# An output projection by block products: seven per pair of token tiles instead of eight

## The chip, the cores and the metric

The kernel runs on one core of a Trainium2 chip. A core has five engines that run side by side, each with its own queue in order: TensorE (PE, matmuls, with a queue of weight loads PEld), VectorE (DVE), ScalarE (ACT), GpSimd (POOL) and SyncE (SP, which here issues all the DMAs). The metric is the device time of one launch in microseconds (us), here the median of three runs.

## The reference

The reference is one layer of a streaming encoder: a modulated RMS norm, one input projection, a state-space branch and an attention branch, and then the output projection, which is what the change touches:

```
mixed = jnp.concatenate([y_ssm, y_att], axis=-1)
y = x + gate[:, None, :] * (mixed @ w_out)
```

`mixed` has 1024 channels (512 of the state-space branch, 512 of attention), for 2048 prompt tokens and 64 decode tokens. `w_out` is 1024 x 1024. All data are float32.

## The kernel before

The program goes through the input projection with the state-space steps between (class `InProj`, `S5`), a gated projection (`Glu`), attention (`Attn`, lines 995 to 1387) and the output projection (`Out`, from line 1480). Both branches leave their outputs, transposed, in DRAM: `ms_d` and `ma_d`, each 512 channels by 2112 tokens.

A float32 product is formed from halves: `split` (line 277) rounds a tile to a high part (float32r) and subtracts it from the tile to get a low part. `mm3` (line 308) then issues three matmuls, high by high, high by low and low by high. A stationary operand is 128 x 128, a moving one 128 x 512.

`Out.weights` (line 1489) is a generator that attention steps through near its end: each step loads a 128 x 512 block of `w_out` into one of three `ost` buffers, rounds it on DVE (`oh`) and subtracts on POOL (`ol`). It takes memory that attention no longer needs. `Out.run` (line 1503) then goes over 17 token tiles, tile 16 (decode) first and then 15 down to 0. For each it loads 128 tokens of `ms_d` and of `ma_d`, splits them on DVE, and for each half of the 1024 output columns runs 8 x 3 matmuls into one accumulator, multiplies by the gate on DVE (line 1531), adds the residual on POOL (`padd`, line 174) and stores.

Attention goes over 20 query tiles, five for each of four pairs of heads. A tile's keys come in blocks, two blocks a group: scores on PE into a `twin`, `p` = exp on ACT (line 304), the sums `acc` over the blocks (line 1297) alternately on DVE and POOL, and one group later the product of `p` with the values (`mix`, into `bank`). At the end of a tile the two `acc` are joined on POOL (line 1379), a matmul against ones sums over the keys (`sums`), and the result `w` is stored to `ma_d` (line 1324). For the very last tile only (`end`), the last six blocks and the join are on DVE (line 1284).

PE's order in attention is the order written (`Chain`, `strict`). Everything else, and the whole output projection, is ordered on each engine by a planner at build time, from estimated costs and dependencies, with the written order as priority. So instructions of the output projection stand among those of attention, as in the first `ost` loads, which go out more than 100 us before attention ends.

## Time and profile before

| | us |
|---|---|
| median of 3 runs | 1456.5 (1455.73 to 1466.12) |
| the profiled execution, whole | 1460.03 |
| its span, first to last instruction | 1458.3 |
| mean granted clock of TensorE | 0.979 |
| first matmul of the output projection | at 1264.94 |
| its last matmul | at 1452.80 |

The profile is of one execution. Times in it count from the first instruction. A group line reads: line, engine, operation, output from inputs, shape, count, then busy time and mean ns of one, then the engine's idle time just before and what ended it. A timeline line reads: start, duration, engine, line, operation, and in brackets the idle time before it and what it waited for. A line of stages gives the stage, then for PE, PEld, DVE, ACT and POOL the busy time and (count), then the granted clock, the DMA share and GB/s. L124 is the helper that all matmuls pass through, so matmuls are told apart by their tiles.

### The profile page before, as it was taken

What the parts mean: (1) busy time and instruction counts of PE and PEld (TensorE: products, weight loads), DVE (VectorE), ACT (ScalarE), POOL (GpSimd) and SP (SyncE); (2) the same over time, 40 slices, a digit from 0 to 9 for tenths busy, and PEclk for the clock granted to TensorE, in tenths of its full rate; (3) what the DMA queues carried; (4) which work ended last, traced back from release to release, by engine and by line L of the source; (5) the groups of instructions that cost most, each with busy time, mean ns of one, the idle gap of its engine ahead of it and who ended that gap; (6) DMA issues with size and microseconds to landing.
All of it is one profiled execution on the core that took longest, in us unless ns stands there. A gap on an engine that the chain in (4) does not pass through costs nothing. (4 is left out here: it accounts for less than half of the span.)

```text
span 1458.3 us, 26193 instructions
## 1 busy us (share of the span) xinstructions
PE 1374.8 (94%) x9730; PEld 1082.7 (74%) x9730; DVE 909.4 (62%) x2406; ACT 541.5 (37%) x1156; POOL 480.5 (33%) x452
## 2 busy tenths in 40 slices
PE   5899989999999999999999999999999897999998
PEld 2798889889888889998878855555555454478887
DVE  2646898678767795564214777886886877342331
ACT  3755215343433444333324435445445344300000
POOL 1101356235322362231125413423324527322222
PEclk9999999999999999999999989999999999999999
DMA  9875423323335725235458623133121222054452
GB/s 336 297 274 150 120 65 85 103 81 89 114 88 165 259 77 139 67 98 148 132 169 252 183 93 107 45 98 93 55 74 38 87 63 91 23 159 147 136 150 94
DMA packets 209383, 184.01 MB, mean 126 GB/s; under 512 B 66823, under 2 KB 169955, under 8 KB 208232
## 3 DMA queue, kind: packets, MB, share of 16 engines
q1 hardware_dynamic: 209256, 182.35, 40.8%
q8 instruction: 76, 1.25, 0.4%
q14 instruction: 51, 0.42, 0.1%
HBM read 125.16 MB, written 57.15 MB: 125 GB/s over the span
## 5 line engine op out<-in xcount | busy, mean ns | idle before, releaser
L124 PE MATMUL low<-whi,h 128*128 128x256 f32 (+1 forms) x2112 | 406.9, 289 | 12.7 <-DVE ev L534 7.3
L124 PEld LDWEIGHTS low<-whi,h 128*128 128x128 f32 x2112 | 337.4, 193 | 23.2 <-issue 11.9
L124 PE MATMUL low<-wlo,h 128*128 128x256 f32 (+1 forms) x1088 | 307.9, 286 | 0.6 <-DVE wlo L284 0.6
L1220 DVE CUSTOM_DVE_ANT_0 pb<-twin,cb 128x512 bf16<-128x512 f32 (+3 forms) x328 | 199.7, 609 | 62.8 <-PE twin L124 51.4
L124 PEld LDWEIGHTS low<-wlo,h 128*128 128x128 f32 x1088 | 209.2, 192 | 2.2 <-issue 1.2
L304 ACT ACTIVATE p<-twin 128x1024 f32<-128x1024 f32 (+3 forms) x180 | 150.0, 839 | 146.1 <-PE twin L124 137.4
L124 PE MATMUL low<-h,whi 128*128 128x512 f32 (+1 forms) x640 | 176.7, 362 | 0.0
L124 PE MATMUL bank<-p,vt 128*64 128x512 f32 (+3 forms) x704 | 143.6, 530 | 0.0
L124 PE MATMUL twin<-qs,ks 64*128 64x512 f32 (+3 forms) x1056 | 134.2, 359 | 0.0
L124 PEld LDWEIGHTS low<-h,whi 128*128 128x128 f32 x640 | 115.0, 192 | 17.7 <-issue 1.7
L290 POOL TENSOR_TENSOR qss<-qss,mhalf 128x4 f32<-128x4 f32 (+1 forms) x68 | 77.2, 1137 | 143.0 <-DVE qss L289 118.9
L124 PE MATMUL low<-h,wlo 128*128 128x512 f32 (+1 forms) x320 | 115.4, 361 | 0.0
L284 DVE TENSOR_TENSOR wlo<-wst,whi 128x512 fp32r<-128x512 f32 (+1 forms) x96 | 67.8, 718 | 76.2 <-ACT whi L282 73.5
L1297 DVE TENSOR_TENSOR acc<-acc,p 128x1024 f32<-128x1024 f32 (+4 forms) x89 | 87.5, 983 | 28.7 <-ACT p L304 27.1
L124 PEld LDWEIGHTS twin<-qs,ks 64*128 64x128 f32 x1056 | 95.2, 191 | 10.9
L124 PE MATMUL twin<-sm,kb 64*128 64x512 f32 (+3 forms) x360 | 78.0, 428 | 17.5 <-DVE pm L1220 17.0
L124 PEld LDWEIGHTS bank<-p,vt 128*64 128x64 f32 x704 | 45.4, 141 | 65.6 <-issue 56.2
L175 POOL TENSOR_TENSOR yo<-yo,x 128x512 f32<-128x512 f32 (+1 forms) x34 | 49.0, 1441 | 133.6 <-DVE yo L1531 133.6
L124 PE MATMUL last<-oh,mh 128*128 128x512 f32 (+1 forms) x208 | 81.4, 391 | 0.0
L124 PE MATMUL last<-ol,mh 128*128 128x512 f32 (+1 forms) x208 | 81.1, 390 | 0.0
L124 PE MATMUL last<-oh,ml 128*128 128x512 f32 (+1 forms) x208 | 81.1, 391 | 0.0
L124 PEld LDWEIGHTS twin<-sm,kb 64*128 64x128 f32 x360 | 34.6, 188 | 60.4 <-DVE pm L1220 40.0
(365 smaller groups left out, 2503.8 us busy)
## 6 DMA issues: line engine op xcount, KB each, us to landing
wst<-in_w_in_dram SPq DMA_DIRECT2D x48, 512.0 KB
h<-h SPq DMA_DIRECT2D x16, 1024.0 KB
wada<-in_w_ada_dram SPq DMA_DIRECT2D x12, 1024.0 KB
cb<-cb_d SPq DMA_DIRECT2D x20, 512.0 KB
x<-in_x_prompt_dram SPq DMA_DIRECT2D x16, 512.0 KB
out_dram<-ev SPq DMA_DIRECT2D x64, 128.0 KB
x<-in_x_prompt_dram SPq DMA_DIRECT2D x32, 256.0 KB
out_dram<-yo SPq DMA_DIRECT2D x32, 256.0 KB
```

What stands on the lines that cost most here:

```text
L124: return self.keep(self.pe.matmul(*a, **kw))
L175: PL.tensor_tensor(out, x, y, op=op)
L284: V.tensor_tensor(lo, x, hi, op=ALU.subtract)
L290: PL.tensor_tensor(out, out, bc(mhalf[:out.shape[0]], list(out.shape)), op=ALU.pow)
L304: i = S.activation(out, x, func, **kw)
L1220: V.tensor_tensor_reduce(b[:, :n], ps[:, h, :n], cb[:, h, :n], 1.0, NEG, ALU.add, ALU.max, accum_out=self.pm[:, t, h, pi:pi + 1])
L1297: (PL if j else V).tensor_tensor(y[:rows, :, c0:nq], x[:rows, :, c0:nq], p[:rows, :, :n], op=ALU.add)
```

## The change

`w_out` is seen as 2 x 2 blocks b11, b12, b21, b22 (512 channels by 512 columns each), and a pair of token tiles with its two branches as 2 x 2 blocks too: a11, a21 (state-space channels of the first and the second tile), a12, a22 (attention channels). Eight block products give the four results. For pairs 1 to 7 the kernel now forms seven, of sums and differences: s1 = a21 + a22, s2 = s1 - a11, s3 = a11 - a21, s4 = a12 - s2 on one side; t1 = b12 - b11, t2 = b22 - b12 + b11, t3 = b22 - b12, t4 = b21 - t2 on the other (`PRODUCTS`). Three accumulators x, y, z are held for a pair, some products add onto what another left, and DVE combines them. Pair 0 is done with four plain products of blocks (`plain`), and the 64 decode tokens with high and low parts side by side in one stationary operand (`decode`).

`w_out` is loaded once as before, rounded now on ACT, and a second time for the sums and differences (`sums`), which `part` splits later; t3 and t4 take the place of b12's halves. Residuals come as whole rows of 1024. A pair's `ms_d` and `ma_d` come in two loads of 256 tokens, issued ahead of the last two stores of the pair before; their buffers are single. High parts of the pairs are rounded on ACT, low parts are on DVE, s1 and s3 on POOL. The pairs run upward, 0 to 7. The last result of the last pair has its residual and an earlier sum added ahead and its last add on DVE.

Inside the output projection the order on each engine is now the written one (`ordered`). In attention, the last two tiles, not only the last, have their last six sums and the join on DVE; the steps of `weights` begin once the last maxima are placed too; and the memory that is free after attention is found by what is in use (`fill`). The core of the diff:

```diff
+    def ordered():
+        start = len(nc.cur_bb.bb.instructions)
+        yield
+        last = {}
+        for i in nc.cur_bb.bb.instructions[start:]:
+            if i.engine in last:
+                tc.add_manual_dep(i, last[i.engine], nosync)
+            last[i.engine] = i.name
...
-                                   given=[False, False], n=0, nb=len(blocks), po=None, end=i == len(self.order) - 1)
+                                   given=[False, False], n=0, nb=len(blocks), po=None, end=i >= len(self.order) - 2)
...
-                if not self.todo and not self.loaded and not self.mx:
+                if not (self.todo or self.loaded or self.mx or self.smq):
...
-        out.mem.add(self.spare("cb", "ks", "qs", "sm", "vt") + self.ring("p", "acc", "z", "w"))
+        out.mem.fill(0, R_AUP[1])
...
+    PRODUCTS = {1: ("x", "a11", "b11"), 2: ("x", "a12", "b21"), 3: ("z", "s4", "b22"), 4: ("y", "a22", "t4"),
+                5: ("z", "s1", "t1"), 6: ("y", "s2", "t2"), 7: ("y", "s3", "t3")}
...
+                st = mem.tile([P, 512], F32, name="ost")
+                e.nc.sync.dma_start(st, self.block(i, j, k))
+                h, l = (mem.tile([P, 512], F32R, name="o%s%d%d%d" % (x, i, j, k)) for x in "hl")
+                e.split(st, h, l)
...
+        self.load(0)
+        for name in ("a11", "a12", "a21", "a22"):
+            self.split(0, name)
+            yield
...
+        for k in range(4):
+            yield from wait(4)
+            for i, j in blocks[1:]:
+                x = self.raw[i, j, k] = mem.tile([P, 512], F32, name="r%d%d%d" % (i, j, k))
+                e.nc.sync.dma_start(x, self.block(i, j, k))
+            b11 = self.raw[0, 0, k] = mem.tile([P, 512], F32, name="ost")
+            e.nc.sync.dma_start(b11, self.block(0, 0, k))
+            self.raw["t", k] = mem.tile([P, 512], F32, name="rt%d" % k)
+            self.sums(k)
+            yield
...
+    def sums(self, k):
...
+        e.V.tensor_tensor(b22, b22, b12, op=ALU.subtract)
+        e.V.tensor_tensor(t2, b22, b11, op=ALU.add)
+        e.padd(b12, b12, b11, ALU.subtract)
+        e.padd(b21, b21, t2, ALU.subtract)
...
+    def part(self, t):
+        for k in range(4):
+            x, lo = self.raw[t, k]
+            if t in ("t3", "t4"):
+                hi = self.b["b12", k][t == "t4"]
+            else:
+                hi = self.mem.tile([P, 512], F32R, name="h%s%d" % (t, k))
+            self.e.split(x, hi, lo, el=None if t == "t3" else self.e.V)
+            self.b[t, k] = hi, lo
...
+    def finish(self, i, n, v, src=None, last=False):
...
+        e.V.tensor_tensor(v[:r], (v if src is None else src)[:r], self.gate[s, n][:r], op=ALU.mult)
+        if last:
+            e.V.tensor_tensor(x, x, v[:r], op=ALU.add)
+        else:
+            e.padd(x, x, v[:r])
+        e.nc.sync.dma_start(e.y_p[t0:t0 + r, ns] if s == 0 else e.y_s[:, ns], x)
...
+        self.multiply(acc, self.a[p, a], b, first)
+        if n == 1:
+            t[p, 1] = self.temp()
+            S.copy(t[p, 1], acc)
+        if n in (1, 6) and (p, 1) in t and (p, "y") in self.acc:
+            t[p, 2] = self.temp()
+            V.tensor_tensor(t[p, 2], self.acc[p, "y"], t[p, 1], op=ALU.add)
+        if n == 7:
+            t[p, 3] = self.temp()
+            V.tensor_tensor(t[p, 3], acc, t[p, 1], op=ALU.add)
+            V.tensor_tensor(t[p, 3], t[p, 3], self.acc[p, "z"], op=ALU.add)
+            self.finish(2 * p + 1, 1, t[p, 3])
...
+        self.residual(16)
+        self.load(1)
+        for i in range(2):
+            self.residual(i)
+        self.decode(1)
+        self.decode(0)
+        self.part("t1")
+        self.differ(1, 1)
+        self.differ(1, 3)
+        self.differ(1, 2)
+        self.differ(1, 4)
+        self.plain(0, 1)
+        self.part("t2")
+        self.plain(0, 0)
+        self.split(1, "s2", "a11", "s1", "a12")
+        self.plain(1, 1)
+        self.part("t3")
+        self.part("t4")
+        self.split(1, "s3", "a22")
+        self.load(2)
+        for i in range(2, 4):
+            self.residual(i)
+        self.plain(1, 0)
+        for p in range(1, 8):
+            q = p + 1 if p < 7 else 0
+            self.split(p, "s4")
+            if q:
+                self.differ(q, 1)
+                self.differ(q, 3)
+            self.product(p, 6)
+            self.product(p, 1)
+            if q:
+                for i in (2 * q, 2 * q + 1):
+                    self.residual(i)
+            self.product(p, 5)
+            if q:
+                self.differ(q, 2)
+                self.differ(q, 4)
+                self.split(q, "s2", "a11")
+            self.product(p, 7)
+            if q:
+                self.split(q, "s1", "a22")
+            self.product(p, 2)
+            if q:
+                self.split(q, "s3", "a12")
+                if q < 7:
+                    self.load(q + 1)
...
+            self.product(p, 3)
+            self.product(p, 4)
```

More of the change, by code (lines that the diff above doesn't have):

```diff
@@ L1485, in __init__ @@
         self.mem = Region(e.nc)
[L1486 to L1487 removed]
+        self.b, self.a, self.x, self.acc, self.tmp, self.raw = {}, {}, {}, {}, {}, {}
+        self.d = []
     def weights(self):
         e = self.e
[L1492 to L1501 removed]
@@ new lines, in split, with multiply @@
+    def split(self, p, *names):
+        for name in names:
+            hi, lo = (self.mem.tile([P, 4, P], F32R, tag="m" + x + name, name="m" + x) for x in "hl")
+            self.e.split(self.a[p, name], hi, lo, el=self.e.V)
+            self.a[p, name] = hi, lo
+    def multiply(self, acc, a, b, first=True):
+        ah, al = a
+        for k in range(4):
+            bh, bl = self.b[b, k]
+            for q, (lhs, rhs) in enumerate(((ah, bh), (ah, bl), (al, bh))):
+                self.e.PE.matmul(acc, lhs[:, k], rhs, start=first and k == q == 0, stop=k == 3 and q == 2,
+                                 skip_group_check=True)
@@ L1615, in body @@
         out.ps = Banks(e.banks(top, "last", 6) + e.psum, *range(8))
-        out.run([16] + list(range(15, -1, -1)))
+        with e.ordered():
+            out.run()
 _INS = ["x_prompt", "x_sample", "cache_k", "cache_v", "cache_logf", "state_ssm_re", "state_ssm_im", "c_prompt",
```

184 lines of the change are left out of this document (142 added, 42 removed).

## The prediction

> **What bounds the kernel now.** I read the page's head first, then the busy time by stages, the chain of waits for the last 300 us, the groups of instructions of the output stage, and the timeline of each engine around the end of attention.
>
> ```profile
> span 1458.3 us, 26193 instructions
> PE 1374.8 (94%) x9730; PEld 1082.7 (74%) x9730; DVE 909.4 (62%) x2406; ACT 541.5 (37%) x1156; POOL 480.5 (33%) x452
> GB/s 336 297 274 150 120 65 85 103 81 89 114 88 165 259 77 139 67 98 148 132 169 252 183 93 107 45 98 93 55 74 38 87 63 91 23 159 147 136 150 94
> 1300.00:1400.00 100.00, 100.00 (x441) 82.50 (x440) 32.50 (x57) 0.00 (x0) 27.05 (x19) 1.00 0.48 145
> 1311.23 32.76 PE last L124 x144
> L124 PE MATMUL last<-oh,mh 128*128 128x512 f32 x192 | 75.0, 391 | 0.0
> L124 PE MATMUL bank<-oh,mh 128*128 128x512 f32 x64 | 25.0, 390 | 0.0
> L124 PE MATMUL last<-oh,mh 128*64 128x512 f32 x16 | 6.4, 398 | 0.0
> ```
>
> The fourth line is a stretch of the output projection: PE is busy for all 100 us at full clock (1.00), DVE for 32.5, POOL for 27, ACT for none, and the DMA engines for 48% at 145 GB/s. So this stage is bound by TensorE, and a matmul left out is time saved. The fifth line, from the chain of waits, prices one: 32.76 / 144 = 0.2275 us (the 391 ns of the groups overlap the next matmul). The last three lines are one operand form each; the forms with ol and with ml have the same counts, so the stage has 3 x (192 + 64 + 16) = 816 matmuls, 185.6 us.
>
> The second place is in attention, ahead of that stage.
>
> ```profile
> 1231.96 0.43 DVE L280 CAST oh<-ost 128x512 fp32r<-128x512 f32 x1 [2.07 <-DMA ost<-in_w_out_dram]
> 1232.30 2.08 DVE L1297 TENSOR_TENSOR acc<-acc,p 128x512 f32<-128x512 f32 x2
> 1232.46 1.64 POOL L175 TENSOR_TENSOR ol<-ost,oh 128x512 fp32r<-128x512 f32 x1 [3.39 <-DVE oh L280]
> 1234.53 2.34 POOL L1379 TENSOR_TENSOR acc<-acc,acc 128x1024 f32<-128x1024 f32 x1 [0.43 <-DVE acc L1297]
> 1236.92 1.98 PE L124 MATMUL bank<-acc,ones 128*64 128x512 f32 x4 [6.39 <-POOL acc L1379]
> 1238.68 3.63 PE L124 MATMUL bank<-p,vt 128*64 128x512 f32 x8
> 1244.30 1.94 PE L124 MATMUL bank<-p,vt 128*64 128x512 f32 x8
> 1268.98 1.03 PE L124 MATMUL bank<-acc,ones 128*64 128x512 f32 x4
> 1237.00:1243.00 6.00, 6.00 (x18) 1.82 (x20) 2.63 (x3) 1.23 (x2) 5.72 (x3) 0.56 0.18 52
> ```
>
> PE stands idle for 6.39 us. Followed back: DVE waits for a block of w_out, rounds it, only then adds the softmax sums of the last but one query tile, POOL splits that block and then joins the two sums, and the matmul against ones waits for it. Afterwards the granted clock is 0.56: the same two groups take 1.98 and 3.63 us instead of 1.03 and 1.94. The place costs 6.4 + 0.95 + 1.69 = 9.0 us. [...]
>
> **The matmuls.** For tokens 256 to 2047 a pair of token tiles takes 7 block products of 12 matmuls instead of 2 x 48: 84 for 96. Tokens 0 to 255 keep four plain blocks of 24. The 64 decode tokens put high and low halves side by side into one stationary operand: 2 x 16 instead of 48. Together 7 x 84 + 96 + 32 = 716 for 816: 100 x 0.2275 = 22.75 us less. All of this counts as long as the operands are ready in time; that is the turnover below.
>
> **The last but one tile.** Its last six blocks and the join go to DVE, and rounding w_out goes from DVE to ACT. POOL's join (2.34 us) and the DVE rounding that held the sums are both off this path. I take the whole 9.0 us, less what ACT brings in:
>
> ```profile
> 1251.32 1.94 ACT L304 ACTIVATE p<-twin 128x1024 f32<-128x1024 f32 x2 [1.91 <-PE twin L124]
> 1239.57 0.63 ACT L304 ACTIVATE w<-w 128x512 f32<-128x512 f32 x1
> PE twin L124 <- DVE pm L1220: 7.6, 9, 2.5
> 1225.35 1.45 DVE L280 CAST oh<-ost 128x512 fp32r<-128x512 f32 x1 [2.29 <-DMA ost<-in_w_out_dram]
> 1240.00:1260.00 20.00, 20.00 (x126) 9.51 (x122) 7.17 (x6) 8.83 (x10) 10.34 (x5) 0.94 0.04 14
> ```
>
> In each group of two key blocks ACT works 1.94 us and idles 1.91 (first line). A copy from SBUF of the same size takes 0.63 (second), so two per group fit: no cost. But ACT runs in order: a copy that waits for its DMA as DVE did (2.29 us, fourth line) holds the exponentials behind it, and PE's next mix waits for those. Ends: 0, and the eight copies of the last eight groups by (2.29 + 0.63 - 1.91) = 8 us. Since a mix runs only after the next group's scores, most of that is covered; I take 1 us. The gain side has an end too: between 1140 and 1270 PE waited 7.6 us, in nine places, for DVE's maxima (third line), and DVE's rounding of w_out stands in that queue; with it gone up to 7.6 us could fall away. I take none, since POOL's halves of the same blocks stay and the order around them is free to change.
>
> **The tail.**
>
> ```profile
> 1452.80 0.39 PE L124 MATMUL last<-oh,ml 128*128 128x512 f32 x1
> 1453.29 0.69 DVE L1531 TENSOR_TENSOR yo<-last,gate 128x512 f32<-128x512 f32 x1 [4.75 <-PE last L124]
> 1454.06 1.26 POOL L175 TENSOR_TENSOR yo<-yo,x 128x512 f32<-128x512 f32 x1 [4.16 <-DVE yo L1531]
> 1455.34 0.34 SPq L1533 DMA_DIRECT2D out_dram<-yo  x1
> ```
>
> Behind the last matmul stand DVE 0.69, POOL 1.26, the store. Now the sum of the last two old terms is done ahead, and the last add is on DVE at 0.69 or less: -0.65 us. The store before it now comes 2.7 us earlier instead of 5.5 us, still ahead of the last one.
>
> **One pair in the steady state.** PE needs 84 x 0.2275 = 19.1 us. What the other engines do beside it:
>
> ```profile
> L284 DVE TENSOR_TENSOR ml<-m,mh 128x512 fp32r<-128x512 f32 x31 | 21.3, 687 | 1.6
> 1289.55 0.68 DVE L1531 TENSOR_TENSOR yo<-last,gate 128x512 f32<-128x512 f32 x1
> 1290.14 0.68 DVE L284 TENSOR_TENSOR ml<-m,mh 128x512 fp32r<-128x512 f32 x1
> 1290.31 1.67 POOL L175 TENSOR_TENSOR yo<-yo,x 128x512 f32<-128x512 f32 x1 [3.08 <-DVE yo L1531]
> 1295.74 1.28 POOL L175 TENSOR_TENSOR yo<-yo,x 128x512 f32<-128x512 f32 x1 [3.76 <-DVE yo L1531]
> 1211.83 2.06 DVE L1297 TENSOR_TENSOR acc<-acc,p 128x1024 f32<-128x1024 f32 x1
> 1244.54 1.23 DVE L1297 TENSOR_TENSOR acc<-acc,p 128x1024 f32<-128x1024 f32 x1 [4.92 <-ACT p L304]
> 1212.76 2.27 POOL L175 TENSOR_TENSOR w<-w,z 128x512 f32<-128x512 f32 x1
> ```
>
> DVE: 7 low halves, 2 differences, 9 combining and gate instructions: 18 x 0.687 = 12.4 us. POOL: 2 differences and 4 residual adds: 6 x 1.28 = 7.7. ACT: 7 high halves and a copy: 8 x 0.63 = 5.0. All are under 19.1. But DVE and POOL delay each other when both read SBUF: an add that POOL does alone in 1.28 took 1.67 beside a DVE subtraction, a DVE add of 1.23 took 2.06 beside POOL. [...] Wholly one after the other they need 20.1 us a pair, 1.0 more than PE; six of DVE's 18 read a PSUM operand, though, so 16.0 is nearer. The first operand that the next pair needs shows the room: product 1 ends 5.5 us into a pair, then come ACT's copy (0.63), DVE's sum, two differences and s2's low half (4 x 0.69), so s2 is ready at about 9 and used at 19.1. So I take 0; ends 0 and 7 x 1.0 = 7.
>
> Accumulators are reused inside a pair: product 7 adds onto a bank that DVE must have read, and products 2, 3 and 4 likewise. Between write and reuse lies at least one product (2.73 us) and the reading needs 0.6 + 0.7: covered. On SP the loads of the next pair stand ahead of the last two stores and behind residual loads that wait for earlier stores; none is needed sooner than about 6 us later.
>
> **The turnover.** Here the change adds most: w_out is read a second time (16 blocks, 4.2 MB), its sums and differences are formed, and four sums are split. PE has cover: 32 decode and 96 plain matmuls, 29.1 us, then three products, 8.2, before the first product 7. DVE and POOL must by then have done, counted from the code: DVE 35 instructions with SBUF operands (4 low halves of pair 0, 8 sums, 4 + 4 + 4 low halves of t1, t2, t4, 2 differences and 7 low halves of pair 1, 2 gate products) and POOL 20 (8 sums, 2 differences, 6 residual adds, 4 low halves of t3).
>
> ```profile
> 1272.71 0.32 SPq L1324 DMA_DIRECT2D ma_d<-w  x1
> 1274.77 0.37 SPq L1513 DMA_DIRECT2D m<-ma_d  x1
> 1277.58 0.49 DVE L280 CAST mh<-m 128x512 fp32r<-128x512 f32 x1 [1.16 <-DMA m<-ma_d]
> ```
>
> 35 x 0.687 + 20 x 1.28 = 49.6 us one after the other against 37.3 of cover. Little of it can be done earlier: in 1240 to 1260 DVE and POOL together were busy 17.5 of 20 us. The second reading can't start in full before attention's buffers are free; at the page's first rate (336 GB/s) its 4.2 MB take 12.5 us, at the output stage's (145) 29. One of the gate loads goes into a buffer that the last attention store must have left (2.1 us from store to next load, first two lines), and pair 1 is queued behind it on SP; a load then takes 2.8 us to its first use. Ends: 0, if work before the turnover and overlap cover the 12.3 us excess, and 15, if nothing does and PE then restarts at 0.56 clock. DVE instructions issued in a row start every 0.59 us (1289.55 and 1290.14 above) rather than 0.69, which takes 3 off the excess; a part of the sums can run in attention's last 15 us. I take 4.
>
> **Sum.** Against the profiled execution (1458.3 span + 1.7 around it = 1460.0): -22.75 - 9.0 - 0.65 + 1 + 4 = -27.4, 1432.6. The median of the runs, 1456.5, is 3.5 below that execution; from it: 1429.
>
> **Rivals.**
> 1. The wait at 1236 only moves: a copy on ACT behind a late w_out block takes 8 to 9 us. For it: the 2.29 us DMA wait that DVE had. Against: the 1.91 us idle in each group. 1429 + 8.5 = 1437.5.
> 2. The turnover starves PE: the whole 15 instead of 4, 1440; with half of ACT's 8 on top, 1444. For it: 49.6 against 37.3. Against: the overlap.
> 3. Attention gives more: with rounding off DVE the earlier waits for maxima go as well. 1429 - 7.6 = 1421.4. For it: one queue. Against: most of those waits stand behind DVE's own maxima, which stay.
> 4. Slower: pair loads have one buffer, so the load of pair q+2 waits for the last low half of pair q+1, and the differences wait for the load. If load (6 us for 1 MB) and 20.1 us of DVE and POOL run strictly in turn, a pair takes 26.1, 7.0 more than PE's: 1429 + 49 = 1478. It decides from 23.0 us a pair, where 7 x 3.9 eats the gain. For it: in-order queues and one buffer. Against: DVE's final combining is not part of the circle, and idle DVE time lies in each pair.
> 5. A saving that doesn't show because the stage is not PE's: the 100 us of 100 speak against it; no chance given.
>
> **How the numbers follow.** Forecast 0.55 (its own range 1424, with nothing lost on ACT or at the turnover, to 1437, with three times the 4), rival 1 0.15, rival 2 0.15, rival 3 0.10, rival 4 0.05. The range 1420 to 1444 holds all but rival 4 and the edges of the others. About 1% (14.6 us) is what a measurement of this kernel can tell from no change, so faster means under 1441.9: forecast, rivals 3 and 1, and a third of rival 2, 0.84; same 0.11; slower 0.05.
>
> **What would show it.** 716 matmuls of the output stage at 0.2275 us; no wait of PE for POOL's join in the last but one tile and no clock of 0.56 there; no PE wait over 1 us from the second pair on; the waits left gathered between decode and the first product 7, under 6 us in all; a last add on DVE. The forecast is wrong if pairs are spaced over 20 us, if the w_out copies stand in front of exponentials with DMA waits, or if PE waits over 10 us at the turnover.

## The result, and the profile after

The changed kernel took 1442.3 us (median of 4 runs, 1441.16 to 1447.4) beside 1457.4 for the kernel before: a ratio of 0.9891, interval 0.9845 to 0.9937. A second series, of the same two kernels once more, gave 1445.38 beside 1455.2: 0.9927, interval 0.9899 to 0.9954. So it is faster by about 1%; whether by more than 1% is not settled. The profiled execution took 1441.16 us.

The page of the changed kernel, span and engines:

```profile
span 1439.4 us, 26171 instructions
PE 1346.0 (94%) x9630; PEld 1060.6 (74%) x9630; DVE 977.4 (68%) x2451; ACT 592.3 (41%) x1252; POOL 516.2 (36%) x476
```

There are 100 matmuls fewer. L143 is now the helper of the matmuls, L303 that of the low halves, L301 that of ACT's high halves. The two profiled spans differ by 18.9 us, but half of that lies ahead of anything the change touches. Here are PE's lines of the timeline, first of the kernel before: the sums of the 14th of the 20 query tiles and the last score of attention.

```profile
1123.25 1.08 PE L124 MATMUL bank<-acc,ones 128*64 128x512 f32 x4
...
1263.13 0.22 PE L124 MATMUL twin<-m_kq,identw 64*128 64x128 bf16 x2
```

And of the changed kernel, these two and then every PE wait of over 1 us from 1206 on, with one line behind the second wait:

```profile
1114.30 1.08 PE L143 MATMUL bank<-acc,ones 128*64 128x512 f32 x4
...
1213.52 0.33 PE L143 MATMUL twin<-sm,kb 64*128 64x128 f32 x2 [1.55 <-ACT p L334]
...
1226.12 0.79 PE L143 MATMUL twin<-sm,kb 64*128 64x512 f32 x2 [4.57 <-ACT p L334]
...
1228.12 1.97 PE L143 MATMUL bank<-acc,ones 128*64 128x512 f32 x4
...
1253.08 0.22 PE L143 MATMUL twin<-m_kq,identw 64*128 64x128 bf16 x2
...
1256.79 0.47 PE L143 MATMUL last<-oh,mhs 128*128 128x512 f32 x1 [1.18 <-DVE mhs L1710]
...
1290.75 0.50 PE L143 MATMUL bank<-ht,mls 128*128 128x512 f32 x1 [2.86 <-DVE mls L303]
...
1305.08 0.80 PE L143 MATMUL bank<-oh,mhs 128*128 128x512 f32 x1 [6.29 <-DVE ot L1684]
...
1314.65 0.50 PE L143 MATMUL last<-oh,mha 128*128 128x512 f32 x1 [1.81 <-DVE ot L1688]
```

Up to about 1138 us both kernels issue the same instructions in the same order on every engine, and yet the 14th sums come 8.95 us earlier. In the eleven later profiles of this study, whose kernels are the same up to there as well, they come anywhere between 1115.11 and 1124.16; the kernel before with one line changed behind that point has 1116.18. So this part varies by some 10 us from execution to execution. Below, every kernel is measured from its own 14th sums to the end of its span: 335.07 us before, 325.15 after, 327.62 in the second profile of the changed kernel. That is a gain of 9.9 and 7.5, not 18.9.

The last six pairs, 504 matmuls, as a stage: first the kernel before, where the last 504 matmuls are the last ten and a half token tiles, then the changed kernel, with the stretch ahead of them and two in attention.

```profile
1338.39:1452.80 114.41, 114.41 (x504) 94.41 (x503) 32.98 (x57) 0.00 (x0) 30.41 (x21) 1.00 0.44 132
```

```profile
1320.23:1434.48 114.25, 114.25 (x504) 94.43 (x503) 86.30 (x104) 23.69 (x41) 53.43 (x36) 1.00 0.45 150
1256.79:1320.23 63.44, 52.48 (x217) 41.25 (x217) 47.29 (x52) 20.05 (x37) 36.80 (x23) 0.95 0.45 149
1220.00:1226.00 6.00, 1.55 (x14) 0.82 (x10) 1.34 (x3) 2.61 (x5) 1.26 (x1) 0.84 0.57 161
1226.00:1252.00 26.00, 25.88 (x150) 12.10 (x152) 11.12 (x10) 13.82 (x17) 13.05 (x6) 0.91 0.20 66
```

In the steady pairs PE is busy in all of 114.25 us at full clock, beside 86.30 of DVE and 53.43 of POOL: the stage is still PE's, and 503 matmul intervals in 114.25 us are 0.2271 each. The first pairs are not: 212 matmuls, worth 48.2 us at 0.2275, take 63.44 (the 217 of the row are these, attention's last four and the one at the border).

| part, us | before | after | second profile | difference | predicted |
|---|---|---|---|---|---|
| 14th sums to last score | 139.89 | 138.78 | 138.55 | -1.1, -1.3 | -8.0 |
| last score to the last 504 matmuls, less 0.2275 for each matmul between | 4.3 | 18.9 | 21.6 | +14.7, +17.4 | +4 |
| matmuls left out | | | | -22.75 | -22.75 |
| the last 504 | 114.41 | 114.25 | 114.25 | -0.2 | 0 |
| last matmul to the end | 5.52 | 4.97 | 4.97 | -0.55 | -0.65 |
| sum | | | | -9.9, -7.5 | -27.4 |

(Second row: before 1338.39 - 1263.13 - 312 x 0.2275; after 1320.23 - 1253.08 - 212 x 0.2275; second profile, whose 14th sums are at 1116.31, 1324.71 - 1254.86 - 212 x 0.2275.) Two terms are off: the stall in attention, and the turnover.

**Attention.** POOL's join is out of the way, as forecast, and there is no wait for it any more. PE waits for ACT instead, 1.55 and 4.57 us. ACT's own timeline just ahead:

```profile
1221.73 0.62 ACT L301 CAST oh<-ost 128x512 fp32r<-128x512 f32 x1 [4.30 <-DMA ost<-in_w_out_dram]
...
1224.01 1.14 ACT L301 CAST mha<-m 128x512 fp32r<-128x512 f32 x2 [1.66 <-DMA m<-ms_d]
1225.06 2.84 ACT L334 ACTIVATE p<-twin 128x1024 f32<-128x1024 f32 x3
```

ACT stands at a copy whose block of w_out has not landed (4.30 us), then at a copy of pair 0's tokens (1.66); the exponentials are queued behind, and PE's scores need the `twin` that they free. PE's last scores before its wait were done at 1221.55 (1226.12 - 4.57), and the first exponential starts at 1225.06, behind both copies: in these rows nothing on ACT passes a copy that waits. Why the block is late stands on SP:

```profile
1218.04 0.33 SPq L1545 DMA_DIRECT2D ost<-in_w_out_dram  x1
```

Its load is issued 0.03 us behind POOL's subtraction of an earlier block, which ends at 1218.01 and frees one of the three `ost` buffers, and it is there 3.7 us later. POOL had itself waited 3.33 us for ACT's rounding of that earlier block. So load, rounding and subtraction follow each other in a circle, and a block isn't asked for before the circle has come round.

The slow clock stays too, 0.84 and then 0.91 for 26 us, and the four matmuls against ones take 1.97 us at a clock of 0.50, much as before (1.98), for the 1.08 of the 14th tile's at 1.00.

**Turnover.** From the changed kernel's timeline, SP, POOL and DVE in order of time:

```profile
1269.05 1.28 POOL L194 TENSOR_TENSOR w<-w,z 128x512 f32<-128x512 f32 x1
...
1270.36 0.32 SPq L1354 DMA_DIRECT2D ma_d<-w  x1
...
1272.38 0.80 SPq L1743 DMA_DIRECT2D gate<-gt_d  x2
...
1273.22 0.48 SPq L1611 DMA_DIRECT2D x<-in_x_sample_dram  x1
...
1274.38 0.51 SPq L1632 DMA_DIRECT2D m<-ma_d  x1
...
1278.63 2.52 POOL L194 TENSOR_TENSOR x<-x,ot 64x512 f32<-64x512 f32 x2 [4.74 <-DMA x<-in_x_sample_dram]
...
1281.67 1.29 POOL L194 TENSOR_TENSOR ms<-m,m 128x512 f32<-128x512 f32 x1 [0.52 <-DMA m<-ma_d]
...
1282.99 0.69 DVE L1644 TENSOR_TENSOR ms<-ms,m 128x512 f32<-128x512 f32 x1 [6.74 <-POOL ms L194]
...
1294.13 5.76 DVE L303 TENSOR_TENSOR r<-r,ol 128x512 fp32r<-128x512 f32 x4
...
1295.90 6.77 POOL L194 TENSOR_TENSOR r<-r,oh 128x512 fp32r<-128x512 f32 x4
...
1304.34 0.68 DVE L1684 TENSOR_TENSOR ot<-bank,ot 128x512 f32<-128x512 f32 x1
```

Read it from the end. Product 7 (1305.08) needs the sum at 1304.34, since it adds onto a bank that this sum reads. DVE has worked without a pause since 1282.99, where it had idled 6.74 us for pair 1's first sum on POOL; POOL had waited for the decode tokens' residual, and that load is on SP behind two gate loads which wait for attention's last store (1270.36), which POOL's last multiplication of attention (1269.05) releases. At 1294 DVE takes 5.76 us for t4's four low halves and POOL 6.77 for t3's; alone they need less: four low halves on DVE took 2.48 us with POOL idle (the run without sums, 1267.55), and one low half on POOL took 1.26 with DVE idle (1222.42), four by that 5.0. So the chain is a late start and then 22 us of work. Which of the two costs what, the experiments below show.

The tail is as forecast, two DVE instructions and no POOL behind the last matmul:

```profile
1434.48 0.39 PE L143 MATMUL last<-ol,mla 128*128 128x512 f32 x1
1434.91 0.69 DVE L1620 TENSOR_TENSOR ot<-last,gate 128x512 f32<-128x512 f32 x1 [1.08 <-PE last L143]
...
1435.69 0.69 DVE L1622 TENSOR_TENSOR x<-x,ot 128x512 f32<-128x512 f32 x1
```

### The profile page after: what moved, and what is told of

It is laid out like the page before. It is cut to its first block, busy times and chain, and to the rows that moved or that the text cites. A ratio compares the mean times of both kernels' runs of the same rounds, so it can differ in the third digit from the quotient of the medians.

```text
span 1439.4 us, 26171 instructions
## 1 busy us (share of the span) xinstructions
PE 1346.0 (94%) x9630; PEld 1060.6 (74%) x9630; DVE 977.4 (68%) x2451; ACT 592.3 (41%) x1252; POOL 516.2 (36%) x476
## 5 line engine op out<-in xcount | busy, mean ns | idle before, releaser
L143 PE MATMUL low<-whi,h 128*128 128x256 f32 (+1 forms) x2112 | 402.4, 287 | 14.4 <-DVE ev L564 10.5
L143 PEld LDWEIGHTS low<-whi,h 128*128 128x128 f32 x2112 | 333.2, 191 | 25.1 <-issue 14.8
L143 PE MATMUL low<-wlo,h 128*128 128x256 f32 (+1 forms) x1088 | 305.6, 284 | 0.5 <-DVE wlo L303 0.5
L143 PEld LDWEIGHTS low<-wlo,h 128*128 128x128 f32 x1088 | 207.0, 190 | 2.3 <-issue 1.2
L143 PE MATMUL low<-h,whi 128*128 128x512 f32 (+1 forms) x640 | 174.0, 357 | 0.0
L143 PE MATMUL bank<-p,vt 128*64 128x512 f32 (+3 forms) x704 | 141.3, 524 | 0.0
L143 PE MATMUL twin<-qs,ks 64*128 64x512 f32 (+3 forms) x1056 | 133.7, 358 | 0.0
L143 PEld LDWEIGHTS low<-h,whi 128*128 128x128 f32 x640 | 112.7, 188 | 17.8 <-issue 1.7
L303 DVE TENSOR_TENSOR wlo<-wst,whi 128x512 fp32r<-128x512 f32 (+1 forms) x96 | 67.7, 718 | 72.7 <-ACT whi L301 70.9
L143 PE MATMUL low<-h,wlo 128*128 128x512 f32 (+1 forms) x320 | 114.0, 356 | 0.0
L143 PEld LDWEIGHTS twin<-qs,ks 64*128 64x128 f32 x1056 | 94.2, 189 | 11.1
L143 PE MATMUL twin<-sm,kb 64*128 64x512 f32 (+3 forms) x360 | 77.4, 425 | 19.2 <-DVE pm L1250 12.6
L143 PEld LDWEIGHTS bank<-p,vt 128*64 128x64 f32 x704 | 44.9, 139 | 64.3 <-issue 56.0
L143 PEld LDWEIGHTS twin<-sm,kb 64*128 64x128 f32 x360 | 34.1, 185 | 60.8 <-DVE pm L1250 34.5
L301 ACT CAST whi<-wst 128x512 fp32r<-128x512 f32 (+1 forms) x96 | 57.5, 621 | 50.7 <-DMA wst<-in_w_in_dram 33.5
L194 POOL TENSOR_TENSOR x<-x,ot 128x512 f32<-128x512 f32 (+1 forms) x34 | 52.2, 1539 | 70.7 <-DVE ot L1620 61.9
L143 PE MATMUL twin<-ks,qs 64*128 64x512 f32 (+3 forms) x328 | 70.3, 432 | 5.1 <-ACT p L334 4.4
L588 DVE SCALAR_TENSOR_TENSOR th<-th,low 128x512 f32<-128x512 f32 (+1 forms) x40 | 23.6, 591 | 70.0 <-ACT th L334 69.7
```

The lines of the kernel that those rows point to most:

```text
L143: return self.keep(self.pe.matmul(*a, **kw))
L194: PL.tensor_tensor(out, x, y, op=op)
L301: S.copy(hi, x)
L303: V.tensor_tensor(lo, x, hi, op=ALU.subtract)
L588: V.scalar_tensor_tensor(th[:, :w], th[:, :w], 1.0, pm[:, :w], op0=ALU.add, op1=ALU.mult)
```

## The experiments

"Stretch" is the time from the first matmul of the output stage to the start of the last six pairs (63.44 and 66.09 us in the two profiles of the changed kernel), "whole" from the 14th sums to the end. The expectations up to the eleventh call the product that waits last "product 2"; it is product 3, which writes the bank that DVE's last sum of product 7 reads.

**The changed kernel once more**, with no edit.

> The changed kernel once more, nothing edited. Between the two profiles shown, 8.95 us of the difference lie ahead of the sums of the 14th query tile (1123.25 before, 1114.30 after), where both kernels have the same instructions in the same order on every engine. Theory (that part differs from execution to execution): here the 14th sums come anywhere from 1114 to 1124, and from them to the end of the span it is again 325 us (before: 335), with the same waits of PE: about 4.6 us in the last but one tile and 12 us between decode and the second pair. The ratio to before is then about 0.993, 10 us. Rival (the part ahead belongs to the change): the 14th sums come at 1114 again and the ratio stays near 0.989.

1445.38 us, ratio 0.9927 (0.9899 to 0.9954), whole 327.62, stretch 66.09. The waits are where they were, with 4.72 and 3.02 us ahead of products 7 and 3 instead of 6.29 and 1.81. The gain in attention is 1.3 us, again small.

**The kernel before, with the last six sums and the join of the last two tiles on DVE**, and nothing else of the change.

```diff
-   ... po=None, end=i == len(self.order) - 1)
+   ... po=None, end=i >= len(self.order) - 2)
```

> The kernel before with one part of the change alone: the last two query tiles, not only the last, have their last six sums and the join on DVE. Theory (the 6.39 us wait came from POOL's join and the low clock from the wait): the wait for POOL's join goes and with it the clock of 0.56; from the 14th sums to the end 335.1 - 9.0 = 326.1 us, and 1457 becomes 1448. Rival (DVE, waiting for a block of w_out at the same place, holds the sums anyway): PE still waits 2 to 5 us there, now for DVE, and no more than 4 us are gained.

1453.17 us, ratio 0.9987 (0.996 to 1.0014); 140.57 us from the 14th sums to the last score, 139.89 without the edit. PE's and DVE's waits in its timeline:

```profile
1228.37 1.08 PE L124 MATMUL bank<-acc,ones 128*64 128x512 f32 x4 [4.06 <-DVE acc L1297]
1231.99 3.68 PE L124 MATMUL bank<-p,vt 128*64 128x512 f32 x8 [2.54 <-DVE z L1312]
```

```profile
1225.89 0.43 DVE L280 CAST oh<-ost 128x512 fp32r<-128x512 f32 x1 [2.31 <-DMA ost<-in_w_out_dram]
...
1230.91 0.43 DVE L280 CAST oh<-ost 128x512 fp32r<-128x512 f32 x1 [2.60 <-DMA ost<-in_w_out_dram]
```

The rival came: the 6.39 us behind POOL's join have become 4.06 and 2.54 behind DVE, 6.60 together. POOL was only the last link; what is late is the block of w_out, and whoever rounds it hands its wait on.

**High halves of w_out and of pair 0 back on DVE**, the rest of the change kept.

```diff
-                e.split(st, h, l)
+                e.split(st, h, l, eh=e.V)
...
-            self.e.split(self.a[p, name], hi, lo, el=self.e.V)
+            self.e.split(self.a[p, name], hi, lo, eh=None if p else self.e.V, el=self.e.V)
```

> All high parts made during attention, of w_out and of pair 0, on DVE as in the kernel before, so that ACT has exponentials alone. Theory (whichever engine rounds w_out waits in order for its loads, and what stands behind is late): no wait of PE for ACT is over 1 us in the last two tiles, but PE waits 3 to 7 us for DVE's sums there, as with the two last tiles on DVE alone (4.06 and 2.54); total within 2 us of the changed kernel. Rival (only ACT is critical): the waits there fall under 1.5 us together and 5 us or more are gained.

1455.44 us, ratio 0.9994 (0.9967 to 1.0021); 144.53 us to the last score, 5.8 more than in the changed kernel.

```profile
1226.41 1.97 PE L143 MATMUL bank<-acc,ones 128*64 128x512 f32 x4 [3.70 <-DVE acc L1327]
...
1235.23 1.12 PE L143 MATMUL bank<-p,vt 128*64 128x512 f32 x2 [6.85 <-DVE z L1342]
```

PE waits for DVE as the theory has it, but longer, 10.55 us together, and the total is 10 to 13 us above that of the changed kernel, where within 2 was expected. So ACT is the better place for the rounding, by about 6 us in attention. With it on DVE the rest of the change makes attention 4.6 us longer than in the kernel before (139.89); which part of it does so was not tried.

**Only pair 0's high halves on DVE** (the second hunk of the diff above).

> The high parts of pair 0 are rounded on DVE instead of ACT; all else as changed. Theory (PE's 4.57 us wait in the last but one tile comes from ACT, which waits in order for the load of pair 0 ahead of an exponential): that wait falls to under 1.5 us, the clock stays at 1.0 behind it, and attention ends 4 to 6 us earlier; if the turnover passes it on, 1442 becomes about 1437. Rival (the blocks of w_out, also rounded on ACT, hold the exponentials as much): the wait stays at 3 us or more.

1443.13 us, ratio 0.9888 (0.9847 to 0.993); 137.11 us to the last score, 1.4 to 1.7 less than in the two profiles of the changed kernel (two later runs, which are equal up to there and share this edit, have 134.81 and 138.01, so that the size is not settled). PE's wait in the last but one tile falls from 4.57 to 2.72 us, between theory (under 1.5) and rival (3 or more), and the whole, 324.42, gains next to nothing: the stretch takes 64.36. ACT still waits for the last block of w_out:

```profile
1228.28 0.62 ACT L301 CAST oh<-ost 128x512 fp32r<-128x512 f32 x1 [4.05 <-DMA ost<-in_w_out_dram]
```

Of ACT's two waits in a row the second goes; the first, for the block, stays.

**A fourth buffer for the blocks of w_out**, with five instead of six `ot` buffers to pay for it.

```diff
-        yield from wait(5)
-        mem.ring("ost", 2048, 3)
+        yield from wait(6)
+        mem.ring("ost", 2048, 4)
```

> Four buffers instead of three for the blocks of w_out, paid for by five temporaries instead of six in the output projection. Theory (ACT waits up to 4.3 us for a block because its load waits for a free buffer, and the exponentials stand behind it): the longest wait of ACT for w_out falls under 2.5 us and PE's wait for ACT in the last but one tile from 4.6 to under 3; the fourth b11 load no longer waits at the turnover, so the wait ahead of product 6 shrinks by 1 to 2 us. Together 2 to 5 us. Rival (what is late is SP's order or the landing itself): the waits stay as they are, within 1 us.

1454.45 us, ratio 0.999 (0.9964 to 1.0016). It doesn't settle the question it was made for: the steps of `weights` begin later, attention takes 146.67 us instead of 138.78, and PE waits 8.4 us for the decode tokens, whose two loads go out at 1263.14 and 1265.67 instead of 1244.05 and 1218.46. ACT's longest wait for a block near the end is 3.30 us for 4.30, PE's for ACT 3.86 for 4.57, both less of a gain than expected (under 2.5 and under 3). Whether a block ordered earlier, with all else in place, would end ACT's wait stays open.

**Pair 1's loads ahead of the gate loads.**

```diff
+        self.load(1)
+        self.residual(16)
+        for i in range(2):
+            self.residual(i)
         for s in (1, 0):
...
-        self.residual(16)
-        self.load(1)
-        for i in range(2):
-            self.residual(i)
```

> In the output projection's written order the loads of pair 1, of the decode residual and of the first two residuals stand ahead of the four gate loads, one of which waits for the last attention store. Theory (the 12 us of PE waits at the turnover start from pair 1 loaded behind that gate load on SP): pair 1 is asked for at 1258 instead of 1273.8, POOL's differences run near 1266 instead of 1281.7, DVE's queue behind them moves up, and of the three waits (2.86, 6.29, 1.81 us) 7 us or more go: 1442 becomes 1435 or less. Rival (DVE and POOL have too much to do there whatever comes when): the differences run earlier but the first product 7 still waits over 5 us, and less than 3 us are gained.

1448.51 us, ratio 0.9936 (0.9913 to 0.996); whole 324.38, stretch 62.74. The loads came early and little followed. DVE's lines of the timeline, and the stage from 1276 to product 7:

```profile
1275.93 0.69 DVE L1589 TENSOR_TENSOR rt<-r,ost 128x512 f32<-128x512 f32 x1 [5.20 <-DMA ost<-in_w_out_dram]
...
1279.96 7.01 DVE L303 TENSOR_TENSOR r<-r,ht 128x512 fp32r<-128x512 f32 x4
```

```profile
1276.00:1308.00 32.00, 23.51 (x103) 18.73 (x102) 31.84 (x30) 11.21 (x21) 22.64 (x14) 0.97 0.21 69
```

DVE now waits for the fourth block of b11, which comes into a buffer that an earlier block must leave; then t1's low halves take 7.01 us beside POOL's sums instead of 3.58, and it is busy in 31.84 of 32 us. Its first difference of pair 1 starts 26.5 us into the output stage, as before (26.2).

**t4's low halves later**, behind product 5 of pair 1.

```diff
-        self.part("t4")
...
+            if p == 1:
+                self.part("t4")
```

> The split of t4 (four copies on ACT, four subtractions on DVE) is written behind product 5 of pair 1 instead of ahead of the last plain product; t4 is first used by that pair's last product. Theory (the 6.3 us wait ahead of product 7 and the 1.8 us wait behind it come from DVE's queue: t4's subtractions, drawn out to 5.8 us beside POOL's t3, stand ahead of the sum that frees the accumulator, and hold back the release of the buffer for pair 2): the two waits, 7.7 to 8.1 us together in the two runs of the changed kernel, fall to 3 us or less, and from the 14th sums to the end it takes 319 to 322 us instead of 325 to 328. Rival (t3 on POOL is what product 7 waits for): the wait stays over 4 us.

1444.07 us, ratio 0.9909 (0.9876 to 0.9943); whole 324.23, stretch 61.97. PE's wait ahead of product 3:

```profile
1322.00 0.56 PE L143 MATMUL last<-oh,mha 128*128 128x512 f32 x1 [4.85 <-DVE ot L1688]
```

Product 7's wait falls from 6.29 to 1.07 (0.36 and 0.71, both for t3 on POOL), product 3's grows from 1.81 to 4.85; 5.9 us together, where 3 or less was expected: the low halves now stand in DVE's queue ahead of product 7's sums.

**Pair 0 on DVE, t4 later and the fourth buffer together.**

> t4 later, four buffers for w_out, and the high parts of pair 0 on DVE, together. If the waits are as the theories have them (4.6 us with about 2.5 of slow clock in the last but one tile, 12 at the turnover), two thirds of them go: from the 14th sums to the end 313 to 318 us, ratio to before about 0.984, 1433. If they only move to another place, 322 or more.

1448.54 us, ratio 0.9956 (0.9932 to 0.998); whole 326.58. This is the second case of the two expected (322 or more). The stretch is the shortest so far, 50.28, but PE waits 7.9 us ahead of it for the decode tokens, time in which DVE and POOL can work ahead, and attention takes 143.94. From the last score to the last six pairs it is 63.4 us, beside 67.1 in the changed kernel, so the turnover gains 3.7 us and not the 13 by which the stretch is shorter; attention's 5.2 more take them away.

**Without most of the sums of w_out's blocks.** It leaves out b12 - b11, b22 - b12 and b21 - t2, so that t1, t3 and t4 are plain blocks.

```diff
-        e.V.tensor_tensor(b22, b22, b12, op=ALU.subtract)
...
-        e.padd(b12, b12, b11, ALU.subtract)
-        e.padd(b21, b21, t2, ALU.subtract)
```

> Leaves out part of the computation: of the sums of w_out's blocks only t2 = b22 + b11 is formed; b12 - b11, b22 - b12 and b21 - t2 are not, so t1, t3 and t4 are plain blocks (4 instructions less on DVE, 8 on POOL; loads, splits, matmuls and their order are as in the changed kernel). Measured from the sums of the 14th query tile to the end (325.2 and 327.6 us in the two profiles of the changed kernel). Theory, DVE and POOL have more to do at the turnover than PE's cover allows: with some 8 x 1.28 + 4 x 0.69 = 13 us of their work gone, the matmuls from the first of the output stage to the start of the last six pairs take 52 to 57 us in place of 63.4 to 66.1, the wait ahead of product 7 of pair 1 (6.29) falls under 2, and the whole to about 316. Rival, the loads behind the gate load come too late whatever DVE and POOL have to do: the waits of product 7 and its neighbours stay, that stretch takes 61 to 66, the whole 324 to 327.

1444.64 us, ratio 0.9901 (0.9861 to 0.9942); whole 319.95, stretch 59.58, between the two expectations. POOL, DVE and PE:

```profile
1263.69 1.29 POOL L194 TENSOR_TENSOR w<-w,z 128x512 f32<-128x512 f32 x1 [16.31 <-ACT w L334]
...
1274.85 2.52 POOL L194 TENSOR_TENSOR x<-x,ot 64x512 f32<-64x512 f32 x2 [9.86 <-DMA x<-in_x_sample_dram]
...
1278.87 0.69 DVE L1641 TENSOR_TENSOR ms<-ms,m 128x512 f32<-128x512 f32 x1 [8.83 <-POOL ms L194]
...
1300.97 0.79 PE L143 MATMUL bank<-oh,mhs 128*128 128x512 f32 x1 [5.36 <-DVE ot L1681]
```

With 13 us of work gone, DVE and POOL idle 8.83 and 9.86 us for the load behind the gate loads, and product 7 still waits 5.36. So the sums cost little as work. They cost by their place: POOL gets to attention's last multiplication 7.0 us after the output stage's first matmul (1263.69 - 1256.73) instead of 12.3 (1269.05 - 1256.79), the store, the gate loads and pair 1 follow it, and DVE's first difference of pair 1 comes 4.1 us sooner.

**Both: earlier loads and a later t4.** Only the two gate loads that wait for attention's last store (s = 0) now stand behind pair 1's loads, and t4 comes behind product 7 of pair 1.

```diff
-        self.residual(16)
-        self.load(1)
+            if s:
+                self.residual(16)
+                self.load(1)
...
-        self.part("t4")
...
             self.product(p, 7)
+            if p == 1:
+                self.part("t4")
```

> Pair 1 and the residuals of the decode tokens are loaded ahead of the two gate loads that wait for attention's last store, and t4 is split behind product 7 of pair 1. Theory (the amount of DVE and POOL work sets the turnover, and a later t4 moves work to where PE has cover): from the first matmul of the output stage to the start of the last six pairs 56 to 60 us instead of 63.4 to 66.1; product 7 and product 2 of pair 1 wait under 2 us each; 1.0 to 1.5% under the kernel before, 321 from the 14th sums to the end. Rival (the wait only moves on to product 4, which then waits for t4): a wait of 3 us or more at product 4 of pair 1, and 324 to 326 as with either edit alone.

1438.3 us, ratio 0.9868 (0.9841 to 0.9895); whole 319.76, stretch 56.52. Product 7 waits 0.27. What is left, on PE and on DVE:

```profile
1309.72 0.69 PE L143 MATMUL last<-oh,mha 128*128 128x512 f32 x1 [3.96 <-DVE ot L1688]
```

```profile
1304.77 0.69 DVE L1644 TENSOR_TENSOR ms<-ms,m 128x512 f32<-128x512 f32 x1 [5.57 <-POOL ms L194]
```

The rival's wait ahead of product 4 did not come, but the one ahead of product 3 did not go either: product 7's sums stand on DVE behind pair 2's difference, which waits for POOL. Nearly the same two edits had shortened the stretch by 0.7 and 1.5 us by themselves, against the first profile; together they take off 6.9.

**That, and pair 0 on DVE, and a buffer of its own for the fourth block of b11.** The buffer takes the memory of one `ot`.

```diff
-            b11 = self.raw[0, 0, k] = mem.tile([P, 512], F32, name="ost")
+            b11 = self.raw[0, 0, k] = mem.tile([P, 512], F32, name="ost" if k < 3 else "osx", bufs=1)
```

> As the kernel with earlier loads and a later t4, and besides the high halves of pair 0 rounded on DVE instead of ACT, and the fourth block of b11 in a buffer of its own rather than in one that an earlier block must leave. Theory (three waits at three places, which add up): attention 1.0 to 1.5 us shorter than in the changed kernel (137 to 138 us from the 14th sums to the last score), the fourth block's sum 2 to 3 us earlier, 54 to 59 us from the first matmul of the output stage to the start of the last six pairs, 319 to 321 from the 14th sums to the end, a ratio of 0.985 to 0.988. Rival (what is taken off one engine's queue comes late on the next): 323 to 326, no different from the changed kernel by more than 2 us.

1434.34 us, ratio 0.9842 (0.9809 to 0.9875), an interval below that of the second series of the changed kernel (0.9899 to 0.9954), with some overlap with the first (0.9845 to 0.9937). Whole 311.59, stretch 52.29, 134.81 us to the last score: each less than expected.

```profile
1303.30 0.50 PE L143 MATMUL last<-oh,mha 128*128 128x512 f32 x1 [2.42 <-DVE ot L1688]
```

Product 7 waits for nothing. Some 3 us of the short attention are scatter, as the next run shows, which is the same up to there and has 138.01.

**Besides, t3's low halves on DVE.**

```diff
-            self.e.split(x, hi, lo, el=None if t == "t3" else self.e.V)
+            self.e.split(x, hi, lo, el=self.e.V)
```

> As the run with all but the memory of the fourth buffers, and the low halves of t3 on DVE instead of POOL. There PE waited 2.42 us ahead of product 3 of pair 1 (the earlier texts call it product 2; it is product 3 that writes the bank which DVE's sum of product 7 reads), that sum stood on DVE behind pair 2's difference, DVE waited 4.13 for it, and POOL could not begin it before t3's low halves (5.94). Theory: POOL is free 3 to 4 us earlier, DVE has idle time for four subtractions of 0.6, product 3's wait falls under 0.5, and the stretch from the first matmul of the output stage to the start of the last six pairs takes 49.5 to 51 in place of 52.3. Rival (DVE is as full as POOL, so that t3 there holds up product 7 as much as it frees product 3): product 7 waits 1.5 us or more, 51.5 to 54.

1434.75 us, ratio 0.9847 (0.9821 to 0.9872), no different from the run before; whole 315.97, stretch 54.73. DVE, SP, POOL and PE:

```profile
1300.25 0.68 DVE L303 TENSOR_TENSOR mla<-m,mha 128x512 fp32r<-128x512 f32 x1
```

```profile
1300.96 0.38 SPq L1632 DMA_DIRECT2D m<-ma_d  x1
```

```profile
1305.96 1.28 POOL L194 TENSOR_TENSOR ms<-m,m 128x512 f32<-128x512 f32 x1 [2.68 <-DMA m<-ma_d]
```

```profile
1312.25 0.60 PE L143 MATMUL last<-oh,mha 128*128 128x512 f32 x1 [3.29 <-DVE ot L1688]
```

Product 7 doesn't wait, against the rival, and POOL is free, as the theory has it; but then POOL waits 2.68 us for pair 2's load. That load goes into the single buffer of pair 1, and it is issued at 1300.96, just as DVE's last low half out of that buffer ends (1300.25 + 0.68); t3's low halves now stand ahead of that one on DVE. Neither was right: the next link was the buffer. The two profiles of the changed kernel differ by 2.65 us in the stretch, so the 2.44 more than in the run before are no loss that this profile could show.

**The turnover in one table.** Times in us from the first matmul of the output stage in each profile; PE alone needs about 38.7 to product 7, as the last two kernels, which don't wait, show.

| kernel | DVE's first difference of pair 1 | from there to product 7 | product 7 | product 7 to 3 | last six pairs |
|---|---|---|---|---|---|
| changed | 26.2 | 22.1 | 48.3 | 9.6 | 63.4 |
| loads first | 26.5 | 21.1 | 47.6 | 9.6 | 62.7 |
| t4 later | 26.7 | 15.9 | 42.5 | 12.3 | 62.0 |
| without sums | 22.1 | 22.1 | 44.2 | 9.8 | 59.6 |
| loads first and t4 later | 24.0 | 14.9 | 38.9 | 10.5 | 56.5 |
| the eleventh run | 20.4 | 18.3 | 38.7 | 8.0 | 52.3 |
| the twelfth run | 20.4 | 18.3 | 38.7 | 8.9 | 54.7 |

The second column is when DVE gets going; the third is what it has to do then, but in the last three rows it ends with PE's own 38.7 and not with DVE's work. An earlier start gives what it is earlier by (the run without sums), a shorter chain gives what it is shorter by (t4 later), and PE's own 38.7 is reached when both are cut. Then the 24 matmuls from product 7 to product 3, 5.5 us of PE's, take 8 to 12: product 7's sums stand on DVE behind pair 2's difference, and that waits for t3's low halves on POOL or for pair 2's load.

## Why the prediction was right and wrong

The time came out in the range, 13 us above the forecast, and the sign was right. It came close, though: by the prediction's own bound faster meant under 1441.9, and 1442.3 is just above; the second series, 1445.38, lies outside the range, which ends at 1444. And of its three signs of being wrong two came: copies of w_out with DMA waits in front of exponentials, and over 10 us of PE's waits at the turnover. By its steps:

- **The matmuls** were right: 716, at 0.2271 us against the 0.2275 reckoned, and the stage stays PE's.
- **One pair in the steady state** was right: no PE wait in the last six pairs, though DVE and POOL are busy 139.7 us in 114.25. So rival 4, the single-buffered loads, did not come as a loop; once, at pair 2, a load waits for the buffer and POOL for the load (2.82 us in the changed kernel, 2.68 in the last run). From the issue of the first of a pair's two loads to POOL's start it is 6.8 us there (1301.58 to 1308.36) and 5.6 in the last run (1300.36 to 1305.96), beside the 6 that the rival took for 1 MB. That DVE's instructions with an accumulator as operand weigh less, for which the step went from 20.1 us a pair to 16.0, has its rows in the changed kernel: an instruction of POOL's took 1.30 us (1326.61) beside a DVE sum that reads an accumulator (1326.53, 0.69), and 1.67 (1333.68) beside low halves of two SBUF tiles (1333.52 and 1334.12, 0.69 and 1.78).
- **The tail** was right, -0.55 for -0.65.
- **The last but one tile** failed, at "I take the whole 9.0 us, less what ACT brings in". The step followed PE's wait back to POOL's join and DVE's rounding and took both off; it named DVE's own wait of 2.07 us for the block, and priced the place as if that wait left with the rounding. The run with that edit alone in the kernel before gained nothing: 6.39 us of wait became 6.60. In the changed kernel ACT waits up to 4.30 us for the block, more than the 2.29 from which the bound of 8 us was made, and exponentials are behind it. This is rival 1, to which 0.15 was given; its 8.5 us less 1.5 is what was lost here (8.0 forecast, 1.1 and 1.3 gained).
- **The turnover** failed, at "I take 4". The step counted 49.6 us of DVE and POOL against 37.3 of cover, an excess of 12.3. What was wrong is the reduction, that starts 0.59 us apart and sums done inside attention would take most of it off. Measured: 14.7 and 17.4 us, at or above the end of 15 that was kept for the range, and of rival 2. Of the 14.7, PE's waits are 12.1 (1.18 + 2.86 + 6.29 + 1.81); the other 2.5 are no waits, and the granted clock is 0.95 in the stretch. That the excess and the waits are so near each other is partly luck, for the excess counts work alone: with 13 us of that work left out the stretch is only 3.9 us shorter (63.44 - 59.58; 6.5 against the second profile). The other part is a start held back by loads behind attention's last store, which the step had named and priced at no term of its own. And DVE and POOL took longer where they met (the rows at 1294 and 1296: 5.76 beside 6.77 us for four each, where DVE took 2.48 with POOL idle and POOL, by 1.26 for one with DVE idle, 5.0).
- **Rival 3**, more gained in attention, did not come.

Rivals 1 and 2 came true together; the nearest case is rival 2's second time, 1444 with the whole 15 and half of ACT's 8. That the time still fell in the range is in part luck, by the runs' scatter: -27.4 + 7 + 11 to 13 is -7 to -10 us, and the first series gave 15.1, the second 9.8.

The eleventh run shows that the lost part could largely be had back in the output stage: from the 14th sums to the end it is 13.6 us shorter than the changed kernel (325.15 - 311.59). The stretch gives 11.2 of it (63.44 - 52.29), attention 4.0, of which some 3 are scatter, and the last six pairs take 1.6 longer (115.82 for 114.25). By the medians, 1434.34 beside 1442.3 and 1445.38, it is 8 to 11 us.

## What to carry to other kernels

A wait that ends at one engine is followed back to what that engine waited for, until a transfer or a compute bound is reached; moving the work off the last link handed the wait on here to whoever took it over (6.39 us for POOL's join became 4.06 and 2.54 for DVE), and on ACT, which took its instructions in order, to all that stood behind (4.30 and 1.66 us of ACT's, then 4.57 of PE's). Where a stage hands over to the next, a late start and a long chain add up, and mending one may show little because the next link takes the wait over (0.7 and 1.5 us by themselves, 6.9 together). When the excess of work over cover has been counted, take nothing off it unless a row shows what hides it, and price a late start as a term of its own; and compare two profiles from the last point at which they still do the same.

## What the hardware showed that was not expected

The first 1114 to 1124 us of these kernels differ by up to 10 us between executions with the same instructions in the same order, as much as the whole effect of the change; a single pair of profiles would have shown it at twice its size. It is PE's busy time that differs, and the granted clock with it. Up to the 14th sums, first the fastest of these profiles (the changed kernel's first), then the slowest (t4 later):

```profile
0.00:1114.30 1114.30, 1051.94 (x7962) 858.72 (x7962) 746.37 (x2093) 480.03 (x1078) 356.06 (x377) 0.99 0.44 134
0.00:1124.16 1124.16, 1065.33 (x7962) 870.70 (x7962) 747.32 (x2093) 480.92 (x1078) 355.78 (x377) 0.97 0.43 133
```

PE is busy 13.4 us longer for the same matmuls, while DVE, ACT and POOL are within 1 us and PE's idle time is no longer (62.4 and 58.8 us). Why the clock is lower in one execution than in another is not shown.

The clock fell behind shorter waits as well. Behind PE's 4.57 us the granted clock was 0.91 on average from 1226 to 1252, and 0.50 in the four matmuls against ones. Behind 3.29 us in the twelfth run matmuls started 0.42 us apart for 3.4 us (1312.25 to 1315.63) and 0.23 from 1316.00 on, and the clock was 0.83 from 1310 to 1320. It was 1.00 in the eleventh run's stretch, whose longest wait was 2.42. The clock did not fall at once behind every wait: in the run with the last two tiles on DVE alone, the four matmuls right behind 4.06 us still took 1.08, and only the eight behind a further 2.54 took 3.68 for 1.94. So two of these waits cost PE more than their own length: the 3.29 us some 1.6 more (8 x (0.4225 - 0.2275)), the 6.39 of the kernel before 2.6 more (0.95 + 1.69).
